# Attention's product with v: one head at a time, high and low part of v side by side as stationary operand

## The chip, the cores and the metric

The kernel runs on one core of one Trainium2 chip. The metric is the device time of one execution in microseconds (us); a median of several runs is given, and one execution is profiled, which yields the trace used here. In the profile the engines are PE (TensorE, matmuls; PEld are its weight loads), DVE (VectorE), ACT (ScalarE), POOL (GpSimd) and SP (SyncE, which issues transfers).

## The reference

Two layers of a bidirectional encoder over 512 tokens of 1024 channels, float32. Each layer adds half a SwiGLU block, then a mixer, then half a SwiGLU block to x; a final RMSNorm ends it. The mixer runs two branches on the same normalized input h, gates them and projects the sum:

```
z = h @ w_in                                  # q, k, v, uf, and two gates
y_na = neighbourhood_attention(q, k, v, rpb) @ w_na_out
y_f  = fourier_mix(uf) @ w_f_out
x    = x + (sigmoid(ga + b0) * y_na + sigmoid(gf + b1) * y_f) @ w_o
```

The attention has 8 heads of 64 channels. The 512 tokens are a grid of 8 rows by 64 columns; a block of 16 query columns (128 queries) sees a band of 32 key columns (256 keys), with a learned bias per relative position and a mask:

```
s = einsum(q, k_win) * scale + bias;  s = where(col_ok, s, -inf)
p = softmax(s)                                # over the 256 keys of the band
o = einsum(p, v_win)
```

So for each head and each of four blocks, o is a product of p (128 queries by 256 keys) with v (256 keys by 64 channels). The change concerns this last product alone.

## The kernel before

All matrix products are made of float32 numbers split in two parts: `hi` is the value rounded to the format that TensorE multiplies (float32r), `lo` is what remains. `split` makes the pair: an ACT copy writes `hi` (L296), a DVE subtraction writes `lo` (L297); with a scale per row it is L299 and L300. `mm3` (L289 to L292) multiplies two pairs with three matmuls into one accumulator: hi with hi (L290), hi with lo (L291), lo with hi (L292). The product of the two low parts is left out.

Weights stream through the whole kernel: a transfer brings a piece (`raw`), ACT writes its high part (`whi`, L181 or L176), DVE its low part (`wlo`, L184 or L177), with three buffers each, prepared ahead of use. The matmul results lie in eight banks of PSUM, given out in turn.

The mixer of a layer is written in this order. `proj_U` and `proj_V` project the Fourier branch's input and v. v is kept with tokens in the partitions: four tiles `vt` of 128 tokens, and, since a band may start at a multiple of 64 in the kernel's order of tokens, three more tiles `vs` shifted by 64, which six SP transfers build from halves of the four (L1206 and L1207). Each tile before holds the high parts of all 512 channels, then the low parts. Then come the Fourier branch's first products, the projections of q and k of head pair 0, and the attention.

The attention runs over eight units i: head pair `hp = i // 2`, and `pr = i % 2`, one half of the four query blocks. A step `att_step(i)` is software-pipelined over three units:

- `att_out(i-2)`: the product of p with v, and the split of its result into `o`
- `att_trans(i-1)`: eight PE transposes (L1051) of the scaled scores into two banks, each split into high and low part of p (`hilo("p")`)
- `att_scores(i)`: the scores (L1019, twelve matmuls), the maximum with bias on DVE (L1029, four instructions), the exponential on ACT (L1035, four, which also sums), two reciprocals (L1038), and the scaling by them on ACT (L1042, four)

Between the steps PE does other work that depends on none of it: the projection of the next q or k (24 matmuls of 512 columns; its result is rotated at L873 and split) for the first five steps, and later two rows of the Fourier branch's output product (`f_rows`: 12 matmuls each, evicted to `fs` at L1106). The last step, 9, has only `att_out(7)`. One row of `f_rows` stands before it and one after it; then comes the product of `o` with its weights (`fill(o, ns, 0, w)`), whose first two weight pieces are split meanwhile, beside sums `t` (L1236, L1238) that a later product needs.

In `att_out` before, one bank takes a unit. The stationary operand is the v of both heads of the pair, 128 channels; the moving operand is p of both heads, 256 columns (2 heads by 128 queries). Of the product, the half in which head and p do not belong together is not used. For two query blocks and two halves of the keys that is 2 x 2 x 3 = 12 matmuls of 256 columns. The result's quarters that belong together are split into `o`: per head, 64 partitions by 256 elements, one ACT and one DVE instruction.

The order of instructions on each engine is made by the framework's scheduler from this program, except where `manual_schedule` fixes it; on-chip buffers come from pools (`slot`: large tiles, `tmp`: the mixer's small ones), and a tile that is taken again waits for its last reader.

Of the kernel before, what the change touches and what calls it, by code (L numbers as in the profile page):

```python
# [9 lines left out]
F32 = mybir.dt.float32  # L10
F32R = mybir.dt.float32r
BF16 = mybir.dt.bfloat16
I32 = mybir.dt.int32
AF = mybir.ActivationFunctionType
ALU = mybir.AluOpType
AX = mybir.AxisListType

P = 128
D = 1024
T = 512  # L20
# [6 lines left out]
NH, DH = 8, 64  # L27
# [6 lines left out]
BAND = (0, 1, 3, 4)  # L34
# [58 lines left out]
def encoder_kernel(  # L93
# [3 lines left out]
    V, S, G, PE = nc.vector, nc.scalar, nc.gpsimd, nc.tensor  # L97
# [11 lines left out]
    def nm(s):  # L109
        uid[0] += 1  # L110
        return f"{s}_{uid[0]}"

    def slot(dt=F32, s="k", shape=(4, 256)):
        return kp.tile([P, *shape], dt, tag="k", name=nm(s), bufs=23)

    def hilo(s):
        t = slot(F32R, s, (2, T))
        return t[:, 0, :], t[:, 1, :]

    def bank(s="ps"):  # L120
        return pp.tile([P, T], F32, tag="ps", name=nm(s))
# [167 lines left out]
    def mm3(ps, lh, ll, rh, rl, start, stop, again=False):  # L289
        PE.matmul(ps, lh, rh, start=start, stop=False, skip_group_check=again)  # L290
        PE.matmul(ps, lh, rl, start=False, stop=False, skip_group_check=again)  # L291
        PE.matmul(ps, ll, rh, start=False, stop=stop, skip_group_check=again)  # L292

    def split(hi, lo, src, scale=None):
        if scale is None:
            S.activation(hi, src, AF.Copy)  # L296
            V.tensor_tensor(lo, src, hi.bitcast(F32), ALU.subtract)  # L297
            return
        S.activation(hi, src, AF.Copy, scale=scale)  # L299
        V.scalar_tensor_tensor(lo, src, scale, hi.bitcast(F32), ALU.mult, ALU.subtract)  # L300
# [531 lines left out]
    def stage_mixer(l, norm, nxt):  # L832
        mp = mix_pool[0]

        def tmp(dt=F32, s="x"):
            return mp.tile([P, T], dt, tag="tmp", name=nm(s), bufs=8)
# [22 lines left out]
        def wide():  # L859

            wh, wl = ws.next()
            for k in range(2):
                c = slice(k * T, (k + 1) * T)
                yield wh[:, c], wl[:, c]
# [58 lines left out]
        def proj_V():  # L923
            pss = [bank() for _ in range(4)]
            for g in range(4):
                for k, (wh, wl) in enumerate(wide()):
                    kt = 2 * g + k
                    for c in range(4):
                        lh, ll = [z[:, c * P : (c + 1) * P] for z in xs[kt]]
                        mm3(pss[c], lh, ll, wh, wl, kt == 0, kt == DT - 1)  # L930
            outs = []
            for c in range(4):
                t = slot(F32R, "v", (2, T))
                split(t[:, 0, :], t[:, 1, :], pss[c], norm.r[:, c : c + 1])
                outs.append(t)
            return outs

# [41 lines left out]
        o, q, k, bms = [], {}, {}, {}  # L979
# [65 lines left out]
        def att_trans(s_):  # L1045
            res = []
            for jj in range(2):
                pt = bank()
                for e in range(2):
                    for c in range(2):  # L1050
                        PE.transpose(  # L1051
                            pt[:, (2 * c + e) * P : (2 * c + e + 1) * P],
                            s_[e][:, jj * 256 + c * P : jj * 256 + (c + 1) * P], ident,
                        )
                hi, lo = hilo("p")
                split(hi, lo, pt)
                res.append((hi, lo))
            return res

        def att_out(i, p_):  # L1060
            hp, pr = divmod(i, 2)
            po = bank()
            hs = slice(hp * P, (hp + 1) * P)
            for jj in range(2):
                ph, pl = p_[jj]
                for c in range(2):
                    vh, vl = vch[BAND[2 * pr + jj] + 2 * c]
                    cs = slice(c * 256, (c + 1) * 256)
                    mm3(po[:, jj * 256 : jj * 256 + 256], vh[:, hs], vl[:, hs], ph[:, cs], pl[:, cs], c == 0, c == 1)
            pv = po.rearrange("p (a e q) -> p a e q", a=2, e=2)  # L1070
            oh, ol = [z[:, pr * 256 : pr * 256 + 256].rearrange("p (a q) -> p a q", a=2) for z in o[hp]]
            for e in range(2):
                r = slice(64 * e, 64 * e + 64)
                split(oh[r], ol[r], pv[r, :, e, :])

        sc, pt_ = {}, {}

        def att_step(i):
            if 0 <= i - 2 < 8:
                att_out(i - 2, pt_.pop(i - 2))  # L1080
            if 0 <= i - 1 < 8:
                pt_[i - 1] = att_trans(sc.pop(i - 1))
            if i < 8:
                sc[i] = att_scores(i)
# [114 lines left out]

        u = proj_U()  # L1200
        vt = proj_V()
        bias_for(0)
        vs = []
        for s in range(3):
            t = slot(F32R, "vs", (2, T))
            nc.sync.dma_start(out=t[0:64].bitcast(F32), in_=vt[s][64:128].bitcast(F32))  # L1206
            nc.sync.dma_start(out=t[64:128].bitcast(F32), in_=vt[s + 1][0:64].bitcast(F32))  # L1207
            vs.append(t)
        vch = {i: (t[:, 0, :], t[:, 1, :]) for i, t in ((0, vt[0]), (1, vs[0]), (2, vt[1]), (3, vs[1]), (4, vt[2]), (5, vs[2]), (6, vt[3]))}
        for g in range(4):  # L1210
            four_pos(g)
        proj_q(0)
# [170 lines left out]
    norm = Norm(0)  # L1383
# [12 lines left out]
    for l in range(L):  # L1396
        nxt = Norm(3 * l + 1)
        stage_ffn(norm, nxt, False)
        norm, nxt = nxt, Norm(3 * l + 2)
        stage_mixer(l, norm, nxt)  # L1400
        norm, nxt = nxt, Norm(3 * l + 3)
        stage_ffn(norm, nxt, l == L - 1)
        norm = nxt
# [130 lines left out]
```

## Time and profile before

| | us |
|---|---|
| median of 3 runs | 1916.05 (1914.85 to 1916.24) |
| profiled execution | 1916.23 |
| its span | 1914.5 |
| PE busy | 1902.0 |
| DVE busy | 1589.1 |
| ACT busy | 1153.0 |
| POOL busy | 188.8 |

The span is the profiled execution from its first to its last instruction. The lines shown further on come from the timeline of one engine: start in us from the span's start, duration in us, engine, line of the kernel, operation, output<-inputs by the program's names, shapes (partitions x elements and type; for a matmul the stationary size first), how many in a row are put together (x4), and in brackets the engine's idle time before it and what ended it. The durations of successive instructions of an engine overlap a little; what an instruction costs its queue is the distance between two starts.

### The profile page before, as it was taken

Reading aid. Unit: us, or ns where it says so; the run is one execution under the profiler, and the core shown is the slowest. Engines: PE = TensorE matmul, PEld = TensorE weight load, DVE = VectorE, ACT = ScalarE, POOL = GpSimd, SP = SyncE. Lnnn points to the kernel's source line nnn. Section 1 sums busy time; section 2 is a strip of 40 time slices with the busy share of each in tenths; the row PEclk is TensorE's granted clock in tenths of the full one; section 3 lists DMA queues with packets and bytes.
Section 4 is the critical chain, followed back from the end, with each engine's and each line's share of the span. In section 5 each row is a group of like instructions: output and inputs, shape, how many; then the busy total and the mean of one; then the engine's idle time right before and its main releaser. Section 6 shows DMA issues by size and latency. Waiting matters only on the chain.

```text
span 1914.5 us, 24707 instructions
## 1 busy us (share of the span) xinstructions
PE 1902.0 (99%) x8997; PEld 1584.0 (83%) x8997; DVE 1589.1 (83%) x1976; ACT 1153.0 (60%) x1670; POOL 188.8 (10%) x234
## 2 busy tenths in 40 slices
PE   9999999999999999999999999999999999999998
PEld 7888888888888888888888888888888888888886
DVE  7878899586989877889977778995769898787899
ACT  6655666457665655566655556663675576555664
POOL 0100010300110011001000100103111100100010
PEclk9999999999999999999999999999999999999999
DMA  9776499321985477649857764974129864766594
GB/s 300 204 212 178 148 257 312 99 69 53 260 219 155 138 192 206 173 155 262 246 146 206 189 176 153 272 271 130 38 94 254 210 165 133 211 175 176 169 277 141
DMA packets 103289, 355.53 MB, mean 186 GB/s; under 512 B 11776, under 2 KB 13952, under 8 KB 103168
## 3 DMA queue, kind: packets, MB, share of 16 engines
q1 hardware_dynamic: 77424, 265.85, 39.8%
q0 software_dynamic: 25600, 88.10, 25.0%
q8 instruction: 70, 1.15, 0.2%
q14 instruction: 51, 0.42, 0.1%
q10 hardware_dynamic: 144, 0.02, 0.0%
HBM read 348.68 MB, written 2.10 MB: 183 GB/s over the span
## 4 chain that ended last, share of the span: by engine, by line
PE 98%; DVE 1%; DMA 0%; ACT 0%; issue 0%; DVEq 0%; ACTq 0%
PE A L451 9%; PE A L452 9%; PE A L454 9%; PE o L452 7%; PE o L451 7%; PE o L454 7%; PE ps L290 5%; PE ps L291 5%; PE ps L292 5%; PE B L451 5%; PE B L452 5%; PE B L454 5%; PE C L452 2%; PE C L451 2%; PE C L454 2%; PE tr L525 2%
## 5 line engine op out<-in xcount | busy, mean ns | idle before, releaser
L184 DVE TENSOR_TENSOR wlo<-raw,whi 128x1024 fp32r<-128x1024 f32 (+1 forms) x522 | 622.8, 1198 | 212.8 <-ACT whi L181 210.9
L181 ACT ACTIVATE whi<-raw 128x1024 fp32r<-128x1024 f32 (+1 forms) x522 | 540.2, 1037 | 421.4 <-PE A L452 128.5
L152 POOL DMA_DIRECT2D raw<-in_wst_dram x152 | 131.1, 868 | 1328.5 <-DMA raw<-in_wst_dram 862.2
L166 DVE TENSOR_TENSOR raw<-raw,raw 128x1024 f32<-128x1024 f32 (+1 forms) x140 | 164.7, 1190 | 1.2
L451 PE MATMUL A<-whi,xh 128*128 128x512 f32 x384 | 149.5, 389 | 0.0
L452 PE MATMUL A<-whi,xl 128*128 128x512 f32 x384 | 149.4, 389 | 0.0
L454 PE MATMUL A<-wlo,xh 128*128 128x512 f32 x384 | 110.5, 389 | 0.0
L177 DVE SCALAR_TENSOR_TENSOR wlo<-raw,whi 128x1024 fp32r<-128x1024 f32 x76 | 89.7, 1192 | 20.4 <-ACT whi L176 20.4
L176 ACT ACTIVATE whi<-raw 128x1024 fp32r<-128x1024 f32 x76 | 78.7, 1035 | 40.9 <-PE cl L452 12.6
L611 ACT ACTIVATE th<-sn,rh 128x512 f32<-128x512 f32 x80 | 57.0, 715 | 73.4 <-DVE sn L507 73.4
L502 ACT ACTIVATE sn<-A 128x512 f32<-128x512 f32 x96 | 56.4, 589 | 54.7 <-PE A L454 54.7
L454 PEld LDWEIGHTS A<-wlo,xh 128*128 128x128 f32 x384 | 72.1, 188 | 14.9
L451 PEld LDWEIGHTS A<-whi,xh 128*128 128x128 f32 x384 | 72.1, 188 | 15.0
L452 PEld LDWEIGHTS A<-whi,xl 128*128 128x128 f32 x384 | 72.1, 188 | 14.9
L451 PE MATMUL B<-whi,t1h 128*128 128x512 f32 x192 | 76.2, 397 | 0.0
L451 PE MATMUL A<-whi,t3h 128*128 128x512 f32 x192 | 75.2, 392 | 0.0
L451 PE MATMUL A<-whi,t2h 128*128 128x512 f32 x192 | 75.2, 392 | 0.0
L451 PE MATMUL C<-whi,xh 128*128 128x512 f32 x192 | 74.9, 390 | 0.0
L452 PE MATMUL B<-whi,t1l 128*128 128x512 f32 x192 | 74.8, 390 | 0.0
L452 PE MATMUL A<-whi,t3l 128*128 128x512 f32 x192 | 74.7, 389 | 0.0
L452 PE MATMUL A<-whi,t2l 128*128 128x512 f32 x192 | 74.7, 389 | 0.0
L451 PE MATMUL B<-whi,xh 128*128 128x512 f32 x192 | 74.7, 389 | 0.0
(362 smaller groups left out, 4747.1 us busy)
## 6 DMA issues: line engine op xcount, KB each, us to landing
raw<-in_wst_dram SPq DMA_DIRECT2D x463, 512.0 KB
raw<-in_wst_dram POOLq DMA_DIRECT2D x156, 512.0 KB, 7.5
raw<-in_wst_dram SPq DMA_DIRECT2D x30, 256.0 KB
vs<-v SPq DMA_DIRECT2D x12, 256.0 KB
bw<-in_rpb_dram SPq DMA_DIRECT2D x32, 68.0 KB
x<-in_xin_dram SPq DMA_DIRECT2D x4, 512.0 KB
raw<-in_wst_dram POOLq DMA_DIRECT2D x8, 256.0 KB, 8.5
dft<-in_dft_dram POOLq DMA_DIRECT2D x8, 256.0 KB, 5.7
```

Of the source, the lines that this page charges most:

```text
L152: G.dma_start(out=self.t, in_=wst[GRAN_AT[self.plus]][:, 0 : self.n], accum_op=ALU.add)
L166: V.tensor_tensor(self.raw.t, self.raw.t, self.add.t, ALU.add)
L176: S.activation(hi, t, AF.Copy, scale=-1.0)
L177: self.last = V.scalar_tensor_tensor(lo, t, -1.0, hi.bitcast(F32), ALU.mult, ALU.subtract)
L181: S.activation(hi[:, cs], t[:, cs], AF.Copy)
L184: self.last = V.tensor_tensor(lo[:, cs], t[:, cs], hi[:, cs].bitcast(F32), ALU.subtract)
L290: PE.matmul(ps, lh, rh, start=start, stop=False, skip_group_check=again)
L291: PE.matmul(ps, lh, rl, start=False, stop=False, skip_group_check=again)
L292: PE.matmul(ps, ll, rh, start=False, stop=stop, skip_group_check=again)
L451: PE.matmul(ps, lh, rh, start=start, stop=False, skip_group_check=again)
L452: PE.matmul(ps, ll, rh, start=False, stop=False, skip_group_check=again)
L454: PE.matmul(ps, lh, rl, start=False, stop=stop, skip_group_check=again)
```

## The change

The two parts of v are stored side by side for each head: 64 channels of the one and 64 of the other make the 128 columns of a stationary operand of one head (high part first in a pair's first head, low part first in its second). The moving operand is this head's p, high and low part as two pieces of 128 columns. One matmul then yields all four partial products of a head (hi hi, hi lo, lo hi and lo lo), in four quarters of the result: the two parts of v in different halves of the partitions, the two parts of p in different columns. Two halves of the keys and two query blocks are four matmuls per head, eight per unit, into one bank for each head.

The parts are then added outside: for each head an ACT copy brings the quarter of v's low and p's high part from the other 64 partitions into this head's 64 partitions of a tile `ot`, and two DVE additions add the two quarters of v's high part to it. The fourth quarter, low by low, is not used. When both heads have been added, one `split` of 128 x 256 writes `o`. `ot` comes from the small pool for units 0 to 6 and from the large one for unit 7.

The split of v has one ACT instruction as before and two DVE instructions, one per head of a pair, in place of one. p's two parts lie in one tile of twice the size.

```
--- before.py
+++ after.py
@@ proj_V
             for c in range(4):
-                t = slot(F32R, "v", (2, T))
-                split(t[:, 0, :], t[:, 1, :], pss[c], norm.r[:, c : c + 1])
+
+                t = slot(F32R, "v", (D,))
+                v_ = t.rearrange("p (h s d) -> p h s d", s=4, d=DH)
+                ps = pss[c].rearrange("p (h e d) -> p h e d", e=2, d=DH)
+                r = norm.r[:, c : c + 1]
+                S.activation(v_[:, :, 0::3, :], ps, AF.Copy, scale=r)
+                for e in range(2):
+                    hi, lo = v_[:, :, 3 * e, :], v_[:, :, 1 + e, :]
+                    V.scalar_tensor_tensor(lo, ps[:, :, e, :], r, hi.bitcast(F32), ALU.mult, ALU.subtract)
                 outs.append(t)
@@ att_trans
-                hi, lo = hilo("p")
-                split(hi, lo, pt)
-                res.append((hi, lo))
+                p2 = slot(F32R, "p", (2, T))
+                split(p2[:, 0, :], p2[:, 1, :], pt)
+                res.append(p2)
             return res
 
         def att_out(i, p_):
             hp, pr = divmod(i, 2)
-            po = bank()
-            hs = slice(hp * P, (hp + 1) * P)
-            for jj in range(2):
-                ph, pl = p_[jj]
-                for c in range(2):
-                    vh, vl = vch[BAND[2 * pr + jj] + 2 * c]
-                    cs = slice(c * 256, (c + 1) * 256)
-                    mm3(po[:, jj * 256 : jj * 256 + 256], vh[:, hs], vl[:, hs], ph[:, cs], pl[:, cs], c == 0, c == 1)
-            pv = po.rearrange("p (a e q) -> p a e q", a=2, e=2)
-            oh, ol = [z[:, pr * 256 : pr * 256 + 256].rearrange("p (a q) -> p a q", a=2) for z in o[hp]]
+            t = tmp(s="ot")[:, 0:256] if i < 7 else slot(F32, "ot", (D,))[:, 0:256]
             for e in range(2):
-                r = slice(64 * e, 64 * e + 64)
-                split(oh[r], ol[r], pv[r, :, e, :])
+
+                po = bank()
+                hs = slice((2 * hp + e) * P, (2 * hp + e + 1) * P)
+                for jj in range(2):
+                    for c in range(2):
+                        v_ = vch[BAND[2 * pr + jj] + 2 * c][:, hs]
+                        z = slice((2 * c + e) * P, (2 * c + e + 1) * P)
+                        PE.matmul(po[:, jj * 256 : jj * 256 + 256], v_, p_[jj][:, :, z], start=c == 0, stop=c == 1)
+                pv = po.rearrange("p (a s q) -> p a s q", a=2, s=2)
+                r, x_ = slice(DH * e, DH * e + DH), slice(DH - DH * e, 2 * DH - DH * e)
+                to = t[r].rearrange("p (a q) -> p a q", a=2)
+                S.activation(to, pv[x_, :, 0, :], AF.Copy)
+                for s_ in range(2):
+                    V.tensor_tensor(to, pv[r, :, s_, :], to, ALU.add)
+            oh, ol = [z[:, pr * 256 : pr * 256 + 256] for z in o[hp]]
+            split(oh, ol, t)
@@ the shifted copies of v
-            t = slot(F32R, "vs", (2, T))
+            t = slot(F32R, "vs", (D,))
...
-        vch = {i: (t[:, 0, :], t[:, 1, :]) for i, t in ((0, vt[0]), (1, vs[0]), (2, vt[1]), (3, vs[1]), (4, vt[2]), (5, vs[2]), (6, vt[3]))}
+        vch = {i: t for i, t in ((0, vt[0]), (1, vs[0]), (2, vt[1]), (3, vs[1]), (4, vt[2]), (5, vs[2]), (6, vt[3]))}
```

## The prediction

> **What bounds the kernel now.** I read the page first, then the timeline of each engine around the attention.
>
> ```profile
> span 1914.5 us, 24707 instructions
> PE 1902.0 (99%) x8997; PEld 1584.0 (83%) x8997; DVE 1589.1 (83%) x1976; ACT 1153.0 (60%) x1670; POOL 188.8 (10%) x234
> PE 98%; DVE 1%; DMA 0%; ACT 0%; issue 0%; DVEq 0%; ACTq 0%
> ```
>
> PE is busy 99% of the span and 98% of the chain that ended last: a matmul taken away is worth its full spacing as long as nothing else is late. So two questions: what do the missing matmuls cost now, and how late are the others at that place? Here is PE in the first layer around one attention step, att_step(3), which runs out(1), then the transposes of step 2, then the scores of step 3 (start, duration, engine, line):
>
> ```profile
> 429.43 0.28 PE L290 MATMUL ps<-p,vs 128*128 128x256 f32 x1
> 429.54 0.28 PE L291 MATMUL ps<-p,vs 128*128 128x256 f32 x1
> ...
> 430.74 0.28 PE L292 MATMUL ps<-p,v 128*128 128x256 f32 x1
> 430.86 1.04 PE L1051 MATMUL ps<-ident,s 128*128 128x128 f32 x8
> 431.83 0.97 PE L1019 MATMUL ps<-q,q 64*128 64x256 f32 x12
> ...
> 439.78 0.49 PE L1051 MATMUL ps<-ident,s 128*128 128x128 f32 x3
> ```
>
> Twelve matmuls take 430.86-429.43 = 1.43 us, 0.12 each. PE comes back to its transposes every 439.78-430.86 = 8.92 us. ACT and DVE in the same stretch:
>
> ```profile
> 428.88 1.70 ACT L1042 ACTIVATE s<-s,rs 128x256 f32<-128x256 f32 x4
> 430.48 1.04 ACT L181 ACTIVATE whi<-raw 128x1024 fp32r<-128x1024 f32 x1
> 431.43 0.61 ACT L296 ACTIVATE q<-q 128x512 fp32r<-128x512 f32 x1
> 432.07 0.38 ACT L296 ACTIVATE o<-ps 64x256 fp32r<-64x256 f32 x1
> 432.35 1.06 ACT L296 ACTIVATE p<-ps 128x512 fp32r<-128x512 f32 x2
> ...
> 435.86 0.51 ACT L1035 ACTIVATE s<-s,nmx 128x256 f32<-128x256 f32 x1 [1.74 <-DVE nmx L1029]
> 437.36 0.49 ACT L1035 ACTIVATE s<-s,nmx 128x256 f32<-128x256 f32 x1
> 437.85 1.69 ACT L1042 ACTIVATE s<-s,rs 128x256 f32<-128x256 f32 x4
> ```
>
> ```profile
> 429.63 0.69 DVE L873 TENSOR_TENSOR q<-ps,R 128x512 f32<-128x512 f32 x1 [0.46 <-PE ps L292]
> 431.56 1.23 DVE L184 TENSOR_TENSOR wlo<-raw,whi 128x1024 fp32r<-128x1024 f32 x1 [1.23 <-ACT whi L181]
> 432.70 0.68 DVE L297 TENSOR_TENSOR q<-q,q 128x512 fp32r<-128x512 f32 x1
> 433.30 0.41 DVE L297 TENSOR_TENSOR o<-ps,o 64x256 fp32r<-64x256 f32 x1
> 433.64 0.67 DVE L297 TENSOR_TENSOR p<-ps,p 128x512 fp32r<-128x512 f32 x1
> 434.34 0.43 DVE L297 TENSOR_TENSOR o<-ps,o 64x256 fp32r<-64x256 f32 x1
> 434.80 0.69 DVE L297 TENSOR_TENSOR p<-ps,p 128x512 fp32r<-128x512 f32 x1
> 435.40 0.41 DVE L1029 CUSTOM_DVE_ANT_0 s<-ps,bm 128x256 f32<-128x256 f32 x1
> ```
>
> This is a closed loop: scales (L1042), whi, wlo, the low parts of q, o, p, then maximum (L1029), exponentials (L1035), scales again. It takes 437.85-428.88 = 8.97 us, as long as PE's own period. The scales end at 428.88+1.70 = 430.58 and the transposes that read them start at 430.86: 0.28 us to spare. Two steps on it is 0.13:
>
> ```profile
> 456.58 0.89 ACT L1042 ACTIVATE s<-s,rs 128x256 f32<-128x256 f32 x2
> 457.60 0.60 PE L1051 MATMUL ps<-ident,s 128*128 128x128 f32 x4
> ```
>
> The second layer runs the same code and shows the same, 0.23 to spare:
>
> ```profile
> 1388.80 1.70 ACT L1042 ACTIVATE s<-s,rs 128x256 f32<-128x256 f32 x4
> 1390.73 1.04 PE L1051 MATMUL ps<-ident,s 128*128 128x128 f32 x8
> ```
>
> So two resources bind here together, PE and the ACT/DVE loop.
>
> **The change, part by part.** *Matmuls.* A step's product with v goes from 12 to 8 matmuls of 256 moving columns. Eight steps, two layers: 64 fewer, at 0.12 us 7.68 us, 3.84 per layer, 0.48 per step. This is the upper bound of the gain. I take 0.12 for the new form too (same columns, same stationary size; its moving operand comes in two pieces of 128). No row has that form; its bounds are 0.12 and, where two pieces would pay as two matmuls of 128 columns, the transposes' (431.83-430.86)/8 = 0.12 each, 0.24: then 8 cost 1.92 instead of 1.43, a loss of 0.49 a step.
>
> *v.* The split of v writes 4x2x64 pieces on ACT (one instruction as now) and two 128x256 on DVE instead of one 128x512, four tiles per layer. An instruction of 256 elements takes 0.42 in this kernel (L1029 above), one of 512 0.68: about 0.16 more each, 0.6 per layer. It is hidden, behind this idle time of DVE some us later, before which the projections keep PE fed:
>
> ```profile
> 398.06 0.69 DVE L873 TENSOR_TENSOR q<-ps,R 128x512 f32<-128x512 f32 x1 [1.53 <-PE ps L292]
> ```
>
> Without that cover it would cost at most 0.6 a layer. The six copies of v rows move the same bytes on SP's queue, with the same orders, and are read first at out(0), behind the projections of q and k: nothing. The split of p only changes where it lies: nothing.
>
> *The evictions.* Before, a step issues on ACT two 64x256 (o) and on DVE two 64x256. After: ACT two copies of 64x256 and one 128x256, DVE four adds of 64x256 and one subtraction of 128x256. ACT gains one (0.38), DVE three (0.42 each, 1.26). The adds start only after out of both heads is done and copied, and they stand in DVE's queue where the maxima, p's low parts and wlo queue behind them. One DVE instruction of 256 elements follows another after 0.34 when nothing is waited for (433.30 to 433.64), 0.46 when what it follows also reads fresh data (434.34 to 434.80). I take 0.36 for the adds, nearest the unhindered row, and keep 0.34 and 0.46 as ends. The added reads of PSUM keep a bank longer; eight banks rotate and PE waits for none of them before.
>
> [...]
>
> *The order.* The built program of the change also has other queues: of each two steps, one computes two maxima before the low parts of o and p, and wlo last; the other keeps the four maxima behind p and puts wlo ahead of the reciprocals that the scales wait for. In both, whi no longer stands ahead of q, but after the copies. I walked one loop of each kind with the spacings above (whi 0.95, wlo 1.14, q 0.63, p 0.53 on ACT and 0.63 on DVE, o low 0.43, maxima 0.345, exponentials 0.495, scales 0.40, copies 0.28, hand-over 0.04). Second kind, from the scales' end: q high 0.67, q low 0.60, adds 1.44, p low 0.63, o low waits 0.3 for its high part behind whi, then 0.43, p low 0.63, four maxima 1.38, wlo 1.14, reciprocals 0.2: 7.41; with the scales' 1.60, 9.01 us. First kind: the exponentials of the first head begin before p's low parts are done, and the loop takes 8.12. Mean 8.57, against PE's new period of 8.92-0.48 = 8.44. So the loop, not PE, sets the steps, and saves 0.35 to 0.40 a step instead of 0.48. Walked over all of a layer's steps (those with rows of the Fourier part in place of projections: 9.24, 8.89, 8.11), PE waits for scales at four transposes, 0.3 to 0.6 us each. When PE reaches the row behind the last transposes, 7 x 0.48 = 3.36 is saved, 1.87 of it waited away: 1.49 left.
>
> *The tail of the layer's attention.* What follows step 8 has no projection to cover it:
>
> ```profile
> 474.00 0.28 PE L290 MATMUL ps<-p,v 128*128 128x256 f32 x1
> ...
> 479.08 0.28 PE L290 MATMUL ps<-p,vs 128*128 128x256 f32 x1
> ...
> 483.26 0.39 PE L290 MATMUL ps<-whi,o 128*128 128x512 f32 x1
> 483.48 0.39 PE L291 MATMUL ps<-wlo,o 128*128 128x512 f32 x1
> ```
>
> ```profile
> 477.88 0.69 DVE L297 TENSOR_TENSOR p<-ps,p 128x512 fp32r<-128x512 f32 x1
> 478.48 1.21 DVE L1236 TENSOR_TENSOR t<-xl 128x1024 f32<-128x1024 f32 x1
> 479.73 1.23 DVE L1238 TENSOR_TENSOR t<-t,t 128x1024 f32<-128x1024 f32 x1
> 481.12 0.42 DVE L297 TENSOR_TENSOR o<-ps,o 64x256 fp32r<-64x256 f32 x1 [0.16 <-ACT o L296]
> 481.46 1.21 DVE L184 TENSOR_TENSOR wlo<-raw,whi 128x1024 fp32r<-128x1024 f32 x1
> ...
> 486.11 1.23 DVE L177 SCALAR_TENSOR_TENSOR wlo<-raw,whi 128x1024 fp32r<-128x1024 f32 x1 [1.23 <-ACT whi L176]
> ```
>
> p's last low part ends at 478.57, out(7) needs it at 479.08: 0.5 to spare. After the change it stands behind four adds (1.44, in place of one o low, 0.43) and one o low, so counted from the start of out(6) it ends at +5.7 instead of 478.57-474.00 = +4.6, while PE is there at 5.08-0.48 = +4.6 (5.08 = 479.08-474.00); my walk has its row behind the transposes 0.1 late, +4.7: a wait of 1.0. Then out(7) saves its 0.48; gain so far 1.49-1.00+0.48 = 0.97. Behind it, first wlo (481.46 to 482.67, needed 483.48: 0.8 to spare) now stands behind copies, four adds, t and one o low: it ends 6.0 after the start of out(7) instead of 482.67-479.08 = 3.6, and the product with o, whose four high matmuls go first, wants it at 483.48-479.08 = 4.40, less 0.48 for out(7), plus 3 x 0.23 for the high matmuls put in front: 4.6. PE waits 1.39. Net of a layer 0.97-1.39 = -0.42, a loss. Behind that, DVE had 1.23 idle at 486.11, so the lateness dies out and PE goes on as before.
>
> **Sum.** The profiled execution took 1916.23 us, 0.18 over the median of the runs shown. Two layers: 2 x (3.84 - 1.87 - 1.00 - 1.39) = 2 x -0.42 = -0.84. 1916.05+0.84 = 1916.9 us: PE has 7.7 us less work and spends it waiting.
>
> **The rivals.** *The loop is shorter than walked, PE gains.* For it: the maxima come earlier in half the steps, DVE is idle 1.23 before wlo at 431.56 and the change fills that. If PE never waited: 1916.05-7.68 = 1908.4. If only the waits in the tail (1.00+1.39) do not occur: 2 x (3.84-1.87) = 3.94, 1912.1. Against: the spare 0.13 to 0.28 at the transposes. It passes 0.2% (3.8 us, about what a measurement of this kernel tells from no change) once 4.7 of the 8.5 us of waits (2 x (1.87+1.00+1.39)) are gone with nothing new: 0.84+3.83. Chance 0.19.
>
> *DVE is the bound, slower.* Its place is the loop and its price 0.1 us per step on six steps and twice in the tail, 0.8 a layer, 1.6 in all. The adds spaced by their whole duration of 0.42, and the low parts of o and p by 0.44 and 0.64 (0.46 and 0.69 are their rows' ends), give, walked, -1.77 per layer, 1919.6. It decides (over 1919.9, 3.0 above my sum) from about 0.2 us per step above my walk, such as adds at 0.46 or ACT's copies across partitions taking more than the 0.38 of the rows: 1920 to 1923. Chance 0.22.
>
> *The change does not shorten the product.* At 0.24 a matmul a step costs 0.49 more, 3.9 a layer; PE's period of 9.41 then covers the loop and p's last low part, and of the first wlo some 0.4 stays uncovered: 2 x 4.3 = 8.6, 1924.7. Against it: the same number of columns goes through. Chance 0.04.
>
> **How the numbers follow.** No measurable change, my forecast, 0.55: 1916.9, own range 1912.3 to 1919.8. Faster 0.19, slower 0.26 (0.22 for DVE, 0.04 for the matmuls). The range leaves out a tenth at either end, below the full saving of PE, above the long matmuls and adds slower than 0.46: 1911.3 to 1921.8.
>
> **What would show it.** PE's busy time down by less than 7.7 us by waits at the transposes (0.3 to 0.6 at the line that answers to L1051), where ACT's scales end last; a wait of about 1 us before the last out of a layer and of about 1.4 before the second group of the product with o, released by DVE. The period of the scales alternates, near 9.0 and 8.1. Wrong, if PE stays without waits (then towards 1908), if each period of the scales is over 9 (then 1920 and up), or if the product with v shows another spacing than 0.12.

## The result, and the profile after

The changed kernel takes 1920.09 us (median of 11 runs, 1919.67 to 1921.95); the kernel before takes 1915.28 us on the same chips (11 runs). The ratio is 1.0024, 95% interval 1.0016 to 1.0032: slower by some 4.6 us, just beyond what can be told from no change. The page of the profiled execution (1920.22 us):

```profile
span 1918.4 us, 24641 instructions
PE 1898.1 (99%) x8933; PEld 1575.9 (82%) x8933; DVE 1606.8 (84%) x2032; ACT 1160.2 (60%) x1686; POOL 192.1 (10%) x234
PE 94%; ACT 3%; DVE 2%; issue 0%; DVEq 0%; ACTq 0%
```

PE has 64 matmuls less (8997 to 8933), and DVE is busy 17.7 us longer. The chain that ended last now runs through ACT and DVE for 5% of the span, where it was PE for 98% before. What PE's matmuls waited for in the attention of the first layer (view of the waits, 415 to 492 us: in all, times, longest); the kernel before has no entry in the same stretch:

```profile
PE ps L1078 <- DVE p L297: 1.6, 1, 1.6
PE ps L1058 <- ACT s L1049: 1.4, 4, 0.4
PE ps L291 <- DVE wlo L184: 1.4, 1, 1.4
```

These are the three places that the prediction named: the last product with v (L1078) waits for p's low part, the transposes (L1058, L1051 before) for the scales, the product with o (L291) for the first low part of its weights. The timeline of PE shows the second of them in one step. From the first two transposes to the other six it is 440.06-439.26 = 0.80 us where 0.24 would do, and the first come 0.15 late, so 0.71 us are lost in all. The view of the waits gives less, 0.36 here, since it counts idle time only:

```profile
438.63 0.40 PE L1078 MATMUL ps<-p,v 128*128 128x256 f32 x2
438.87 0.40 PE L1078 MATMUL ps<-p,vs 128*128 128x256 f32 x2
439.26 0.44 PE L1058 MATMUL ps<-ident,s 128*128 128x128 f32 x2
440.06 0.88 PE L1058 MATMUL ps<-ident,s 128*128 128x128 f32 x6 [0.36 <-ACT s L1049]
440.87 0.39 PE L1026 MATMUL ps<-q,q 64*128 64x256 f32 x2
```

Pairs of the new matmuls follow each other after 438.87-438.63 = 0.24, so one costs 0.12 as assumed. And this is the loop that the transposes wait for, ACT's scales and DVE between them:

```profile
429.53 1.69 ACT L1049 ACTIVATE s<-s,rs 128x256 f32<-128x256 f32 x4
431.13 0.61 ACT L296 ACTIVATE q<-q 128x512 fp32r<-128x512 f32 x1
...
438.70 1.71 ACT L1049 ACTIVATE s<-s,rs 128x256 f32<-128x256 f32 x4 [0.27 <-DVE rs L1045]
```

```profile
431.77 0.69 DVE L297 TENSOR_TENSOR q<-q,q 128x512 fp32r<-128x512 f32 x1 [1.36 <-ACT q L296]
432.38 1.77 DVE L1084 TENSOR_TENSOR ot<-ps,ot 64x256 f32<-64x256 f32 x4
434.19 0.69 DVE L297 TENSOR_TENSOR p<-ps,p 128x512 fp32r<-128x512 f32 x1
434.94 0.42 DVE L297 TENSOR_TENSOR o<-ot,o 128x256 fp32r<-128x256 f32 x1
435.28 0.68 DVE L297 TENSOR_TENSOR p<-ps,p 128x512 fp32r<-128x512 f32 x1
435.88 0.42 DVE L1036 CUSTOM_DVE_ANT_0 s<-ps,bm 128x256 f32<-128x256 f32 x1
...
437.26 1.33 DVE L184 TENSOR_TENSOR wlo<-raw,whi 128x1024 fp32r<-128x1024 f32 x1
438.52 0.21 DVE L1045 RECIPROCAL rs<-sm 128x2 f32<-128x2 f32 x2
```

From 431.77 on DVE has no gap above 0.06: the period, 438.70-429.53 = 9.17 us, is a sum of DVE instructions behind ACT's scales and the high part of q. The four additions take 434.19-432.38 = 1.81 us of it. The next period is 447.14-438.70 = 8.44; the mean of six is (473.95-419.99)/6 = 8.99, and PE alone could do with 8.92-0.48 = 8.44.

In the tail of the layer (PE, then DVE):

```profile
474.19 0.40 PE L1078 MATMUL ps<-p,v 128*128 128x256 f32 x2
...
478.56 0.39 PE L292 MATMUL ps<-whi,y 128*128 128x512 f32 x1
480.54 0.74 PE L1078 MATMUL ps<-p,vs 128*128 128x256 f32 x4 [1.59 <-DVE p L297]
...
484.35 1.07 PE L290 MATMUL ps<-whi,o 128*128 128x512 f32 x4
486.77 0.50 PE L291 MATMUL ps<-wlo,o 128*128 128x512 f32 x1 [1.35 <-DVE wlo L184]
```

```profile
477.04 1.78 DVE L1084 TENSOR_TENSOR ot<-ps,ot 64x256 f32<-64x256 f32 x4 [1.68 <-ACT ot L1082]
479.31 0.42 DVE L297 TENSOR_TENSOR o<-ot,o 128x256 fp32r<-128x256 f32 x1 [0.48 <-ACT o L296]
479.79 1.29 DVE L297 TENSOR_TENSOR p<-ps,p 128x512 fp32r<-128x512 f32 x2
481.00 1.22 DVE L1248 TENSOR_TENSOR t<-xl 128x1024 f32<-128x1024 f32 x1
482.20 1.78 DVE L1084 TENSOR_TENSOR ot<-ps,ot 64x256 f32<-64x256 f32 x4
484.02 1.23 DVE L1250 TENSOR_TENSOR t<-t,t 128x1024 f32<-128x1024 f32 x1
485.16 0.42 DVE L297 TENSOR_TENSOR o<-ot,o 128x256 fp32r<-128x256 f32 x1
485.49 2.35 DVE L184 TENSOR_TENSOR wlo<-raw,whi 128x1024 fp32r<-128x1024 f32 x2
```

p's low parts stand behind the additions of the unit before, and the first low part of the weights of o behind those of the last. Measured against the kernel before at the same instructions, the first layer is 0.08 us late at its first scores, 0.29 early at the last transposes, 1.46 late at the last product with v, and 2.78 late when the gates' product begins; the second layer loses another 2.65 to that point. Behind each, 0.6 to 0.8 us come back.

### The profile page after: what moved, and what is told of

Read it like the earlier page. It is cut to its first block, busy times and chain, and to the rows that moved or that the text cites. A ratio compares the mean times of both kernels' runs of the same rounds, so it can differ in the third digit from the quotient of the medians.

```text
span 1918.4 us, 24641 instructions
## 1 busy us (share of the span) xinstructions
PE 1898.1 (99%) x8933; PEld 1575.9 (82%) x8933; DVE 1606.8 (84%) x2032; ACT 1160.2 (60%) x1686; POOL 192.1 (10%) x234
## 4 chain that ended last, share of the span: by engine, by line
PE 94%; ACT 3%; DVE 2%; issue 0%; DVEq 0%; ACTq 0%
PE A L451 9%; PE A L454 9%; PE A L452 9%; PE o L451 7%; PE o L452 7%; PE o L454 7%; PE B L451 5%; PE B L452 5%; PE B L454 5%; PE ps L291 4%; PE ps L292 4%; PE ps L290 4%; PE C L451 2%; PE C L452 2%; PE C L454 2%; PE tr L525 2%
## 5 line engine op out<-in xcount | busy, mean ns | idle before, releaser
L451 PE MATMUL A<-whi,xh 128*128 128x512 f32 x384 | 149.4, 389 | 0.0
L502 ACT ACTIVATE sn<-A 128x512 f32<-128x512 f32 x96 | 56.4, 589 | 55.2 <-PE A L454 55.2
L451 PEld LDWEIGHTS A<-whi,xh 128*128 128x128 f32 x384 | 72.1, 188 | 15.0
L451 PE MATMUL B<-whi,t1h 128*128 128x512 f32 x192 | 76.1, 397 | 0.0
L451 PE MATMUL A<-whi,t3h 128*128 128x512 f32 x192 | 75.2, 392 | 0.0
L451 PE MATMUL A<-whi,t2h 128*128 128x512 f32 x192 | 75.2, 392 | 0.0
L451 PE MATMUL C<-whi,xh 128*128 128x512 f32 x192 | 74.9, 390 | 0.0
L452 PE MATMUL C<-whi,xl 128*128 128x512 f32 x192 | 74.7, 389 | 0.0
```

The source lines that it names most:

```text
L452: PE.matmul(ps, ll, rh, start=False, stop=False, skip_group_check=again)
```

## The experiments

Each kernel ran on one chip together with the kernel before; ratios are to that, with 95% intervals. The kernel before had 1916.23 us with e1 to e4, 1915.33 with e5 to e8 and 1916.22 with e9 to e12.

**e1, no additions.**

```
...
-                S.activation(to, pv[x_, :, 0, :], AF.Copy)
-                for s_ in range(2):
-                    V.tensor_tensor(to, pv[r, :, s_, :], to, ALU.add)
...
-            split(oh, ol, t)
...
+                split(oh[r], ol[r], pv[r, :, 0, :])
```

> The changed kernel without the copies and additions behind the product with v: each head's quarter of high v by high p alone is split into o, with two ACT and two DVE instructions of 64x256 as in the kernel before (the other quarters are left out of the result). Theory, the additions fill DVE's queue: the loop of scales comes back to its mean period before, about 8.7 us, PE's waits at the transposes shrink to under 0.3 us, the waits before the last out (1.75 us) and before the first low part of the weights of o (1.5 us) go: 1910 to 1912.5 us. Rival one, PE alone bounds without the additions: all 64 matmuls are gained, 1907.6. Rival two, the new form of matmul itself costs more than it saves: no gain, 1915 or more.

1909.38 us, ratio 0.9965 (0.9952 to 0.9977): 6.85 us faster than before, of the 7.68 that the matmuls are worth. PE's waits, same view and stretch as above:

```profile
PE ps L1058 <- ACT s L1049: 0.3, 1, 0.3
```

So the new matmuls do save what they were to save, and the additions with their copies take all of it and 4 to 5 us more. As a gain it is nearer to the first rival (7.68) than to my theory: the loop is no floor of 8.7 us. Without additions its mean period falls to (471.15-419.92)/6 = 8.54.

**e2, no additions in the last two units of a layer** (the same edit for i > 5).

> The changed kernel with the additions left out for the last two units of a layer only (units 6 and 7, whose o then has the product of the high parts alone). Theory, two of the three waits stand in the tail: the 1.75 us before the last out fall below 0.4, the 1.5 us before the low part of the weights of o below 0.5, the transposes before keep their 0.6 us waits; 2 x (2.4 to 3.2) less than 1920.1: 1913.7 to 1915.3 us. Rival, the tail only collects lateness of the steps ahead of it: the waits stay and the time is over 1918.5.

1914.38 us, ratio 0.9991 (0.9982 to 1.0). Both waits of the tail are gone and the waits at the transposes stay (1.5 us, four times): about 6.3 us of the cost (1.0024 less 0.9991) are the additions of two units of eight. The other 5 us (0.9991 less 0.9965) are those of the six before.

**e3, PE's share undone.**

```
-                        PE.matmul(po[:, jj * 256 : jj * 256 + 256], v_, p_[jj][:, :, z], start=c == 0, stop=c == 1)
+                        for n in range(1 + c):
+                            PE.matmul(
+                                po[:, jj * 256 : jj * 256 + 256], v_, p_[jj][:, :, z], start=c == 0, stop=c == 1 and n == 1
+                            )
```

> The changed kernel with PE's share undone: the four matmuls of the second half of the keys are issued twice, so that a step has 12 of them again (o then counts that half twice). Theory, ACT and DVE set the steps and PE only waits for them: the 0.48 us per step go into waits that are there, 1920 to 1922 us. Rival, PE still bounds and something else made the kernel slower: 1920.1 + 64 x 0.12 = 1927.8 us.

1925.72 us, ratio 1.0047 (1.0035 to 1.006): 4.4 us over the changed kernel, between theory and rival. The scheduler also placed DVE's work of two steps differently. The six periods of the scales tell it apart: 9.54, 9.17, 8.44, 9.28, 9.10, 8.43 in the changed kernel, 9.93, 9.18, 9.99, 9.30, 9.19, 8.42 here. Four are the same within 0.1 in spite of 0.48 us more PE work in each; the two that grew are those whose queue changed. In the steps the theory holds, but the run does not test it cleanly.

**e4, additions on the same partitions.**

```
-                S.activation(v_[:, :, 0::3, :], ps, AF.Copy, scale=r)
+                S.activation(v_[:, :, 0::2, :], ps, AF.Copy, scale=r)
...
-                    hi, lo = v_[:, :, 3 * e, :], v_[:, :, 1 + e, :]
+                    hi, lo = v_[:, :, 2 * e, :], v_[:, :, 2 * e + 1, :]
...
-                to = t[r].rearrange("p (a q) -> p a q", a=2)
-                S.activation(to, pv[x_, :, 0, :], AF.Copy)
-                for s_ in range(2):
-                    V.tensor_tensor(to, pv[r, :, s_, :], to, ALU.add)
...
+                to = t[0:DH, e * 256 : e * 256 + 256].rearrange("p (a q) -> p a q", a=2)
+                S.activation(to, pv[DH : 2 * DH, :, 0, :], AF.Copy)
+                V.tensor_tensor(to, pv[0:DH, :, 0, :], to, ALU.add)
+                V.tensor_tensor(t[r, 0:256].rearrange("p (a q) -> p a q", a=2), pv[0:DH, :, 1, :], to, ALU.add)
```

> The changed kernel with high part before low part for both heads, so that three of the four additions of a step read and write partitions 0 to 63 and only the last of a unit writes the upper half for the second head; as many instructions as before it, of the same size. In the changed kernel an addition follows the one before it after 0.44 to 0.46 us, though 0.42 long. Theory one, an instruction waits for the end of the one in front when it starts at other partitions: additions within the lower half follow after 0.34, about 0.2 less per step, 1916.5 to 1918.5 us. Theory two, the spacing comes from the addition in place or from the waits that each carries: 0.45 as before and 1920 us.

1918.14 us, ratio 1.0011 (1.0002 to 1.002): by the ratios 2.5 us less than the changed kernel, though the two intervals overlap a little (1.0016 to 1.002), so that the size is uncertain. DVE in one step, the first additions of both heads (L1083), the second ones (L1084):

```profile
441.02 0.74 DVE L1083 TENSOR_TENSOR ot<-ps,ot 64x256 f32<-64x256 f32 x2
441.69 0.85 DVE L1084 TENSOR_TENSOR ot<-ps,ot 64x256 f32<-64x256 f32 x2
442.57 0.43 DVE L1036 CUSTOM_DVE_ANT_0 s<-ps,bm 128x256 f32<-128x256 f32 x1
```

An addition of 0.41 us that is followed by one at the same partitions is followed after 0.33 to 0.34; ahead of the last, which writes the upper half, and of what comes behind it, 0.44 to 0.45. In the changed kernel the additions of a step stand in the same order, first ones of both heads, then second ones, so that they alternate between the heads' halves, and the spacings are 0.44 to 0.46. So theory one holds for them: it is the start partition.

One case is left over. In the first step of a layer the second head's copy comes late, and a head's two additions follow each other directly, the second reading the sum that the first writes. In e4 both are at the same partitions:

```profile
421.86 0.42 DVE L1083 TENSOR_TENSOR ot<-ps,ot 64x256 f32<-64x256 f32 x1 [0.69 <-ACT ot L1082]
422.31 0.42 DVE L1084 TENSOR_TENSOR ot<-ps,ot 64x256 f32<-64x256 f32 x1
```

They are 0.45 apart all the same. So an addition right behind the one whose sum it reads costs that much too; in the other steps the other head's addition stands between them.

**e5, p's split first; e6, the maxima first; e7, a tail in order by hand; e8, e7 with e4's layout.** The same instructions in other places of the program; `evict` holds the copies, additions and split of o, which `att_out` now returns, and lines that begin with # are remarks:

```
             if 0 <= i - 2 < 8:
-                att_out(i - 2, pt_.pop(i - 2))
+                evict = att_out(i - 2, pt_.pop(i - 2))
             if 0 <= i - 1 < 8:
                 pt_[i - 1] = att_trans(sc.pop(i - 1))
# e5: the next two lines here
+            if 0 <= i - 2 < 8:
+                evict()
             if i < 8:
                 sc[i] = att_scores(i)
# e6, e7, e8: these two lines here instead
...
# e7, e8:
+        with tc.manual_schedule(engines={mybir.EngineType.DVE, mybir.EngineType.Activation}):
+            ws.prep(ws.pos + 1)
+            att_step(9)
```

(e7 and e8 have att_step(8) in such a block too.)

> The changed kernel with one edit of order: a step emits its copies, additions and split of o behind the transposes and the split of p instead of ahead of them; the scheduler places them from there, still ahead of most of the maxima. Same instructions. Theory, what costs is where the additions stand: p's low parts of the last unit no longer wait for them, so the 1.75 us before the last out fall below 0.4, while the loop of scales keeps its additions ahead of the maxima and its waits, and the first low part of the weights of o still comes late: 0.5 to 1.7 us per layer, 1917 to 1919.5 us. Rival, DVE simply has too much work for PE's shorter step wherever it stands: no change, 1919.5 to 1921.

> The changed kernel with the copies, additions and split of o emitted behind the scores' maxima and exponentials of the step as well; the scheduler then has most additions behind the reciprocals. Same instructions. Theory, position: the loop of scales no longer holds the additions, the 0.6 us waits at the transposes go below 0.2 (about 3 us a layer), the tail keeps part of its two waits: 1912 to 1916 us. Rival, amount of work: DVE has 1.4 us more a step, the period of the scales stays at 9.0 and the time over 1918.

> As e6, and in the tail an order of ACT and DVE written out by hand: in step 8 p's splits ahead of the additions, in step 9 the split of the first weights of o ahead of the additions of the last unit. Same instructions. Theory: both tail waits fall below 0.5 us, nothing is left of the 12.6 us of waits but some tenths, and the saving of PE shows: 1909 to 1912 us. Rival: the additions come late for what follows them, the product with o waits for o itself instead: over 1914.

> As e7, with the layout of e4 (three additions of four within the lower 64 partitions, 0.2 us less per step on DVE). Theory: by now DVE's queue is not what PE waits for, so the shorter additions bring little, 0 to 1 us less than e7. Rival: DVE's work still bounds, 2.5 us less as in e4.

None is faster than the changed kernel (1.0024, 1.0016 to 1.0032): 1921.79 (1.0036, 1.0023 to 1.0048), 1924.19 (1.0047, 1.0034 to 1.0059), 1928.63 (1.0072, 1.006 to 1.0085), 1924.49 (1.0047, 1.0033 to 1.0061); e5's interval overlaps with it. My expectations failed, and the traces say why. In e5 the wait before the last product with v is gone as expected, but the lateness moves on. ACT's queue has the high part of the last o, which waits for the additions, ahead of the high part of the weights of o:

```profile
483.32 0.42 ACT L296 ACTIVATE o<-ot 128x256 fp32r<-128x256 f32 x1 [2.15 <-DVE ot L1088]
483.65 0.58 ACT L1126 ACTIVATE fs<-ps 128x512 f32<-128x512 f32 x1
484.12 1.05 ACT L181 ACTIVATE whi<-raw 128x1024 fp32r<-128x1024 f32 x1
```

```profile
485.22 0.96 PE L290 MATMUL ps<-whi,o 128*128 128x512 f32 x3 [2.48 <-ACT whi L181]
```

In e6 the additions hold their PSUM banks longer, and the scores, which take the next bank, wait for them:

```profile
469.13 1.05 PE L1026 MATMUL ps<-q,q 64*128 64x256 f32 x9 [1.38 <-DVE ot L1088]
```

The e6 wait recurs in e7 (1.4 us) and e8 (1.1 us), and the product with o waits 2.1 and 1.9 us for ACT there. Behind the attention of e7 and e8 stands one more wait in each layer that the changed kernel has not: a later product (L451) waits for ACT (L502), 3.5 us in all in e7 and 2.9 in e8. So e7 and e8 do not show the cost of the additions' place alone. e8 against e7 is 0.25% faster: DVE's work still counts. Whether another order would free the saving was not settled; these four do not.

**e9, e11, e12, low parts of the weights on POOL; e10, the last two units as before.**

```
+                    on = G if self.raw.key[1:2] == ("f",) or self.raw.key[1:] in [("qk", g) for g in range(4, 8)] else V
-                    self.last = V.tensor_tensor(lo[:, cs], t[:, cs], hi[:, cs].bitcast(F32), ALU.subtract)
+                    self.last = on.tensor_tensor(lo[:, cs], t[:, cs], hi[:, cs].bitcast(F32), ALU.subtract)
...
-                att_out(i - 2, pt_.pop(i - 2))
+                (att_out if i < 8 else att_out_1)(i - 2, pt_.pop(i - 2))  # e10, e11; att_out_1: the form before
```

> The changed kernel with eight low parts of weights per layer (those of the last four projections and of the Fourier rows, one a step, 1.1 us of DVE) moved from DVE to POOL; additions, order of the program and PE as in it. Theory, DVE's queue of the attention steps is full and its work sets the period of the scales: with 1.1 us less a step the waits at the transposes (0.6 us in four steps of seven) go, 2 to 3 us a layer; the two waits of the tail stay: 1914 to 1917 us. Rival, the place of the additions alone counts, not the amount of work: the waits stay, 1919 to 1921. Risk named beforehand: POOL takes about 0.72 us per 128x256, so some 3 us for one low part; if PE waits for them, over 1922.

> Units 0 to 5 in the changed form with the layout of e4, units 6 and 7 (the last two of a layer) as before the change: twelve matmuls, two splits of 64x256, v of the last head pair stored high parts first. Theory: against e4 (1918.1) the tail loses its two waits (1.4 and 1.3 us a layer) and gets back 2 x 0.48 of PE, so 2 x 1.7 less: 1914 to 1916, level with the kernel before or just under it. Rival, the tail's waits come from lateness collected in the steps: over 1917.

> e10 with the eight low parts of weights on POOL as in e9. Theory: neither transposes nor tail wait, and the saving of PE on six units shows, 2 x 6 x 0.48 = 5.8 us: 1909.5 to 1912 us, faster than both kernels. Rival as in e9.

> The kernel before with the eight low parts of weights on POOL as in e9: what that move does by itself. Theory: PE bounds the kernel before and waits for nothing in the attention, so nothing is gained: 1914.5 to 1916.5 us. Rival: a gain of over 2 us, by which e11 would owe its time to this move and not to the change.

e9 has 1938.43 us (1.0117, 1.0102 to 1.0133), e11 1930.5 (1.0074, 1.0062 to 1.0087), e12, the kernel before with this one edit, 1928.95 (1.0066, 1.0053 to 1.0078). The control explains it. POOL and then DVE in e12:

```profile
435.40 2.40 POOL L185 TENSOR_TENSOR wlo<-raw,whi 128x1024 fp32r<-128x1024 f32 x1 [7.79 <-ACT whi L181]
```

```profile
435.82 2.52 DVE L298 TENSOR_TENSOR q<-q,q 128x512 fp32r<-128x512 f32 x1 [2.31 <-ACT q L297]
438.26 0.41 DVE L298 TENSOR_TENSOR o<-ps,o 64x256 fp32r<-64x256 f32 x1
```

DVE's instruction, 0.68 long in the kernel before, ends 0.54 us after POOL's. So it was held up while POOL worked: the two ran side by side for 1.98 us, and it took 1.84 us more. All eight of these instructions in e12 took 2.0 to 2.5 us. Nothing was taken off DVE, whose busy time is 1592.4 us against 1589.1 in the kernel before. These three runs therefore tell nothing of the theory they were made for.

e10 has 1916.8 us, 1.0004 (0.9995 to 1.0012), level with the kernel before, just above the top of what I expected. In its first layer PE waits nowhere in the tail and 0.7 us in all at the transposes, yet at the last transposes it is 0.96 us behind the kernel before, 0.61 of them from ahead of the first scores, which its longer split of v may explain; that was not tested. The other 0.35, and the 2.88 us that the six changed units save up to there, are lost in the steps: the period of the scales has a mean of (474.90-419.87)/6 = 9.17, longer than the 8.99 of the changed kernel, and the view of the waits shows only a part of it. No version that ran beats the kernel before with its whole computation done.

## Why the prediction was right or wrong

The forecast was 1916.9 us, no measurable change, with 1912.3 to 1919.8 of its own; 1920.09 lies outside that and inside the whole range, 1911.3 to 1921.8. What came is the rival "DVE is the bound", at the lower edge of its 1920 to 1923.

- *Matmuls*: right. 0.12 us each in the new form, and e1 realises 6.85 of the 7.68 us. "The change does not shorten the product" falls.
- *v costs nothing*: right. The first scores start at 406.37 instead of 406.30.
- *The places*: right in the main. All waits that the walk put at the transposes, before the last out and before the second group of the product with o are there, in that order and with those releasers, and nowhere else before the kernel's attention ends. The two kinds of period are there too, 9.17 and 8.44 (forecast: 9.0 and 8.1), then 9.28, 9.10 and 8.43 (9.24, 8.89, 8.11). The first of the six, 9.54, is of neither kind: DVE still waits 0.67 for the first copy, and its fourth addition stands behind wlo (425.39).
- *The size of the additions*: this is the step that failed. "I take 0.36 for the adds, nearest the unhindered row, and keep 0.34 and 0.46 as ends": it is 0.45. The four additions cost 1.81 us a step instead of 1.44, and 1.81 stands once in each period and twice in the tail's chain. Measured terms in the first layer: the transposes wait 2.99 us instead of 1.87 (3.36 saved less 0.29 and 0.08), the last out 1.75 instead of 1.00 (480.54-478.79, where PE is ready), the weights of o 1.51 instead of 1.39. 2 x (3.84-2.99-1.75-1.51) = -4.8 instead of -0.84; 1915.28+4.8 is 1920.1. That this meets the median so closely is in part luck: in the profiled pair the small gaps add some 0.6 to the lateness and 1.4 come back behind the attention, and the last matmul is 4.0 us late.
- *Why the wrong end of a bounded price*: the two rows that bounded it (0.34 and 0.46) were both splits of o followed by p. I told them apart by what they read; the difference was that the second head's lies in the upper 64 partitions. e4 shows it on the additions themselves: 0.33 to 0.34 at the same partitions, 0.44 to 0.45 at others.
- *What the price was worth*: e4 also weighs the step. Its four additions take 433.47-431.91 = 1.56 instead of 1.81, and the three waits of the first layer fall from 2.99+1.75+1.51 = 6.25 us to 2.26+1.43+1.25 = 4.94 (first scores 0.22 and last transposes 1.32 ahead of the kernel before; 479.17-477.74 and 485.14-483.89). At that rate the 0.37 by which the price was short would make 1.94 us a layer, an estimate; the forecast's waits were short by 6.25-4.26 = 1.99. So by this estimate the price of the additions accounts for nearly all of the miss. The estimate puts all of e4's gain down to the additions, though e4 brings ACT's two copies closer together as well (0.28 apart instead of 0.41).
- *The tail's walk*: its 1.00 was wrong in other terms too, which in part cancelled. The additions of unit 6 begin 477.04-474.19 = 2.85 us after the start of its product, where the first low part of o began 476.04-474.00 = 2.04 after it in the kernel before; the low part of o waits 0.48 for its high part (479.31); and PE goes on at 480.54, when only the first of p's two low parts is done.
- *"Two resources bind here together"*: half right. In the kernel before ACT and DVE's loop was as long as PE's period because PE's results set its pace; e1 shows it running at 8.54. With the additions in it, it does bind.
- *The rival's threshold*: right in its example, "such as adds at 0.46", too steep in its price. Adds at 0.46 are 0.4 us a step above the walk, not 0.2; and at 1.6 us in all for each 0.1 a step, the 0.37 measured would have added 5.9 us, where 4.8-0.8 = 4.0 came on top of the forecast.
- *Whether the amount of DVE's work or its place decides*: that the amount counts is shown, by e4 and by e8 against e7. Whether a better place would do without it is open: e5 to e8 moved the additions and found other waits instead; e9 and e11 did not lighten DVE.

## What to carry to other kernels

Here a matmul saved (0.12 us) by leaving a sum to the vector engines was paid per instruction there (0.45 us an addition on DVE); count those instructions in the loop that feeds PE, and price them by rows with the same pattern of partitions, not by the cheapest row of the same size (0.34 here). Additions that alternate between two halves of the partitions cost 0.45 us here, at one half 0.33, and 0.45 again where one read the sum of the one right in front of it. Putting late work later brought new waits (1.38 us for a PSUM bank in e6, 2.48 for ACT's queue in e5) four times out of four: before reordering, list what holds a bank and what stands behind the moved instruction on both engines.

## What the runs showed of the hardware

- DVE overlapped an instruction of 256 elements with the next by some 0.08 us when both started at the same partitions (0.41 long, 0.33 apart), and not at all when they did not (0.03 between them), nor in e4's first step, where the second reads what the first writes (0.42 long, 0.45 apart).
- ACT showed the first of these too: the two copies of a step are 0.41 apart in the changed kernel, where they read and write different halves (476.63 0.78 x2, each 0.38 long), and 0.28 in e4, where both read the upper and write the lower half (475.38 0.66 x2). In the changed kernel the first copy of the first layer, which writes the lower half, is followed after 0.28 by the high part of q, which starts there too (421.71).
- POOL's subtraction of 128x1024 (2.40 us) held up the DVE instruction that started beside it in e12, the low part of q of 128x512, until it had ended (0.68 became 2.52).
- In e6 PE ran at about half speed for some us behind its longest wait in the first layer (2.0 us). The windows there (columns: stretch and length, busy time and count of PE, PEld, DVE, ACT, POOL, granted clock, DMA share, GB/s):

```profile
487.00:490.50 3.50, 3.50 (x10) 2.63 (x10) 3.02 (x4) 2.24 (x3) 1.76 (x2) 0.53 1.03 410
490.50:494.00 3.50, 3.50 (x17) 2.92 (x16) 3.47 (x4) 0.00 (x0) 0.00 (x1) 1.00 1.05 324
```

At the clock of 0.53 successive matmuls of 512 columns start 0.43 apart (488.42, 488.85), at 1.00 it is 0.23 (490.66, 490.89): the ten from 486.46 to 490.44 take 3.98 us where 2.3 would do, so some 1.7 us are lost beside the wait. Behind e5's wait of 2.5 us in the first layer matmuls followed each other after 0.23 (487.52, 487.75), and in the changed kernel the clock stayed at 1.00 behind waits of 1.6 and 1.4 us, so this adds to e6 and not to the result above.
